# Low part of the next split weight tile given out ahead of the last step's evacuation

## The chip, the cores and the metric

The kernel runs on one core of one Trainium2 chip. The metric is the device time of one execution in microseconds (us), lower is better. Before the change it is 2506.51 us, the median of three runs (2506.17 to 2506.94).

## The reference

Two blocks over 256 tokens of width 2048, all in float32. Cut to what matters here:

```
# first block
proj   = rms_norm(x) @ w_in                       # 2048 -> 8192: q k v, h b c, z_conv z_attn
y_conv = rms_norm(b * conv3(c * h)) * silu(z_conv)
y_attn = rms_norm(attention(norm(q), norm(k), v)) * silu(z_attn)
x      = x + concat(y_conv, y_attn) @ w_out
# second block
proj   = rmsnorm(x) @ w_in_2                      # conv input, ssm input, two gates
conv   = silu(layernorm(conv31(glu))) @ conv_w_out_2
ssm    = (z @ w_val) * sigmoid(z @ w_gate),  z = gelu(scan of the grouped state space)
x      = x + (gate0 * conv + gate1 * ssm) @ w_out_2
h      = rmsnorm(x)
x      = x + peer(h)        # q = h @ w_q; top 16 of 128 x 128 keys; 16 experts' rows of u and v per head
out    = rmsnorm(x)
```

## The kernel before, in words

The 256 tokens stand on the free axis; the width is cut into rows of 128 partitions. The program goes through a list of 448 weight tiles of 128 x 2048 (1 MB each). The first 192 tiles are the projections; each of them is **split**. A raw tile comes by DMA on SP's queue into one of three buffers (RAW). ScalarE (ACT) copies it, rounded to fp32r, into one of three HI buffers: the high part (`w_hi`, L195). VectorE (DVE) subtracts that from the raw tile into one of two LO buffers: the low part (`w_lo`, L201). TensorE then multiplies high part by high input, high part by low input and low part by high input, which together give nearly the full float32 precision. The first two products stand in one matmul of 512 columns where the step is "wide" (L301, and L302 for the low part), or in three matmuls of 256 columns (L286 to L288, L277 to L279). The last 256 tiles (expert tables) are **whole**: their steps use the raw tile, without high or low part.

One tile is one step, given out by `step(mm, evac)` in one manually scheduled program, so each engine's queue has exactly the order in which the code gives the work out:

1. the pending evacuation of the step before, out of PSUM (`pend`);
2. `w_ahead(i)`: loads into free raw buffers, the low part of tile i+1 (with `LDL = 1`), the high part of tile i+2 (with `LDH = 2`);
3. the matmuls of step i;
4. a share of other work from generators (`weave`): attention, the state-space scan, the long convolution, square roots.

The load of tile i+4 goes out after the low part of tile i+1, whose raw buffer it takes. The low part of tile i+1 overwrites that of tile i-1, so it also waits for the matmuls of step i-1.

The evacuations differ by stage. In the wide steps `total` copies one half of the PSUM bank by ACT (L311) and adds the other half by DVE (L313):

- **query and key steps** (`ev_q`, `ev_k`; 16 of the first 24 tiles): L311, L313, then a square on ACT (L506, L521). For a key, later in the weave: square root on ACT (L530), reciprocal (L532) and scaling (L533) on DVE. Between them, `q_scale` (L562 on ACT, L564 and L565 on DVE).
- **value, h, c and b steps**: L311, L313, with nothing on ACT behind DVE for v and h; c multiplies (L627) and runs a three-tap convolution in the weave; b multiplies (L647) and squares on ACT (L649).
- **gated z steps** (`ev_z`, 16): L311, L313, scaling L668 beside silu on ACT (L666), product L670, then `split_to`: copy on ACT (L343), subtraction on DVE (L344).
- **residual steps** (`residual_step`, 16 in each block): L311, L313, addition L844, square on ACT (L850); in the second block also `split_x`: copy on ACT (L1147) and L1148 on DVE.
- **projections of the second block** (L1064 to L1078): ACT alone, or for glu ACT and then a product on DVE.
- **value-gate steps** (`ev_vg`): sigmoid on ACT (L1111), two products on DVE (L1112, L1113).
- **c-out steps** (`ev_co`, 8): twice product, addition (L1120, L1121) on DVE, copy on ACT (L343), subtraction on DVE (L344).
- **query projections of the last stage** (`ev_pq`): one product on DVE (L1166).

Of the kernel before, what the change touches and what calls it, by code (L numbers as in the profile page):

```python
# [123 lines left out]
def body(ctx, tc, xT, par, wst, kst, bblk, cblk, gfin, uexp, vexp, out):  # L124
# [28 lines left out]
    LDH, LDL = 2, 1  # L153
    WU = 192
    ws = {"n": 0, "dma": 0, "hi": 0, "lo": 0}
    order = []
# [8 lines left out]
    def raw_of(i):  # L165
        return RAW[i % 3] if i < WU else EARLY[i - WU] if i < WU + 3 else S[w_slot[i]]
# [11 lines left out]
    def w_release(i):  # L178

        k = w_slot.pop(i, None)  # L180
        if k is not None:
            w_free.append(k)
# [9 lines left out]
    def w_hi():  # L192
        i = ws["hi"]
        if i not in whole:
            nc.scalar.activation(hi_of(i), raw_of(i), AF.Copy)  # L195
        ws["hi"] += 1

    def w_lo():
        i = ws["lo"]
        if i not in whole:  # L200
            nc.vector.tensor_tensor(out=lo_of(i), in0=raw_of(i), in1=FV(hi_of(i)), op=ALU.subtract)  # L201
        ws["lo"] += 1

    def w_loads():
        while ws["dma"] < len(order) and raw_free(ws["dma"]):
            w_load()

    def w_ahead(i):

        last = len(order) - 1  # L210
        w_loads()
        while ws["lo"] <= min(i + LDL, last) and ws["dma"] > ws["lo"]:
            if ws["hi"] <= ws["lo"]:
                w_hi()
            w_lo()
            w_loads()
        while ws["hi"] <= min(i + LDH, last) and ws["dma"] > ws["hi"]:
            w_hi()

    plain = lambda raw: raw  # L220
    w_base = {"q": 32, "k": 40, "v": 48, "h": 0, "b": 8, "c": 16, "zc": 24, "za": 56}
# [29 lines left out]
    def step(mm, evac, budget=2600.0, fine=0.0):  # L251

        i = ws["n"]
        while pend:
            pend.pop(0)()
        w_ahead(i)
        parts = mm(raw_of(i)) if i in whole else mm(hi_of(i), lo_of(i))
        for _ in parts or ():
            weave.run_fine(fine)
        ws["n"] += 1  # L260
        if i in whole:
            w_release(i)
        pend.append(evac)
        weave.run(budget)
        weave.run_paced()
# [151 lines left out]
    def first_tiles(pss, xs, evs):  # L417

        i, n = ws["n"], len(pss)
        w_ahead(i)  # L420
        ws["n"] += n
        his, los = [[w[j % len(w)] for j in range(i, i + n)] for w in (HI, LO)]
        wk = lambda w, k: w[:, k * P:(k + 1) * P]
        late = list(range(1, KT, 2)) + list(range(0, KT, 2))
        jobs = [(his[t], t, k, 0) for k in range(KT) for t in range(2)]
        if n == 2:
            jobs = [j for k in range(KT) for j in ((his[0], 0, k, 0), (los[0], 0, k, 0), (his[1], 1, k, 0))]
            jobs += [(his[t], t, k, 1) for t in range(2) for k in late] + [(los[1], 1, k, 0) for k in range(KT)]
        else:
            jobs += [(his[t], t, k, 1) for k in late for t in range(2)]  # L430
            jobs += [(his[2], 2, k, p) for p in range(2) for k in range(KT)]
            jobs += [(los[t], t, k, 0) for t in range(3) for k in range(KT)]
        for q, (w, t, k, p) in enumerate(jobs):
            if ws["lo"] < i + n and t == 1 and w is los[1]:
                w_lo()
            rest = [u for _, u, _, _ in jobs[q + 1:]]
            nc.tensor.matmul(pss[t], wk(w, k), xs(k)[p], start=all(u != t for _, u, _, _ in jobs[:q]),  # L437
                             stop=t not in rest)
        if n == 3:
            w_hi()  # L440
            w_lo()
            w_loads()
        pend.extend(evs)
        weave.run(0)
# [375 lines left out]
    for kind, j in plan[3:]:  # L820
        ps = mmbank2(1)
        if kind == "k" and j == 0:
            weave.add(q_scale(), True)
        if kind == "h" and j == 0:
            for g in range(3):
                weave.add(attention(g), True)
        ev = {
            "q": lambda: ev_q(ps, j), "k": lambda: ev_k(ps, j), "v": lambda: ev_v(ps, j),
            "h": lambda: ev_copy(ps, sl(u_s, j)), "c": lambda: ev_c(ps, j), "b": lambda: ev_b(ps, j),
            "za": lambda: ev_z(ps, a_s, col["aog"], rbuf, j, 8 + j),  # L830
            "zc": lambda: ev_z(ps, u_s, col["cog"], rconv, j, j),
        }[kind]()
        if kind == "za" and j == 0:
            weave.drain()
            y_s = slots([18, 19, 20, 17], F32R)
            yv = hl_view(y_s)
        step(lambda wh, wl: mm_wide(ps, wh, wl, hl2(h_s), range(KT)), ev)
# [4 lines left out]
    def residual_step(ps, j, xsv, ysv, perm, then=lambda j: None, last=lambda f: f()):  # L842
        def ev():
            nc.vector.tensor_tensor(out=xsv(j), in0=total(ps), in1=xsv(j), op=ALU.add)  # L844
            if j == 0:
                nc.scalar.activation(sqsum, xsv(j), AF.Square)
                then(j)
                return
            sq = hold()
            nc.scalar.activation(sq, xsv(j), AF.Square)  # L850
            if j < KT - 1:
                nc.gpsimd.tensor_tensor(out=sqsum, in0=sqsum, in1=sq, op=ALU.add)  # L852
            then(j)
            if j == KT - 1:
                def f():
                    sum_tokens(sqsum, True, False)
                    sum_tokens(sq, False, True)
                    drop(sq)
                last(f)
            else:  # L860
                drop(sq)
        if j == KT - 1:
            need_sqrt()
        step(lambda wh, wl: mm_wide(ps, wh, wl, ysv, perm), ev)
# [221 lines left out]
    for j in range(2, 8):  # L1086
        ps = mmbank()
        step(proj(ps), ev_u(ps, j), mix())
# [635 lines left out]

    n0 = ws["n"]
    w_ahead(n0 + LAST - 1)
    ws["n"] += LAST
    zs = slots([9, 23])
# [113 lines left out]
```

## Time and profile before

| | |
|---|---|
| median of 3 runs | 2506.51 us |
| the profiled execution | 2509.01 us, of it the span from first to last instruction 2507.0 us |
| TensorE (PE) busy | 2405.0 us, 96% of the span |
| weight loads (PEld) busy | 2279.6 us |
| VectorE (DVE) busy | 1616.7 us |
| ScalarE (ACT) busy | 729.1 us |
| GpSimd (POOL) busy | 642.4 us |
| low part L201, 192 times | 453.3 us, 2362 ns each |
| high part L195, 192 times | 366.1 us, 1908 ns each |
| mean granted TensorE clock | 0.994 |

The split stages fill the first 1220 us or so; the rest are the steps with whole tiles. TensorE is busy nearly all the time, so what matters is what it waits for in the few per cent that are left, and whether VectorE and ScalarE have the next high and low parts ready when a step begins. In a timeline row the first number is the start in us, the second the duration; in brackets at its end is how long the engine sat idle before, and what ended that.

### The profile page before, as it was taken

To read this page: it belongs to the slowest core of one execution; us is meant where nothing else is said; L and a number is where in the kernel's file an instruction comes from. 1 tells how busy PE (TensorE), PEld (TensorE's weight loads), DVE (VectorE), ACT (ScalarE), POOL (GpSimd) and SP (SyncE) were. 2 spreads that over 40 slices of the span, in tenths; PEclk is the share of its full clock that TensorE was granted. 3 is DMA by queue.
4 is the path that set the end of the run, shared out by engine and by line. 5 is a ranking of instruction groups with operands and counts; after the bars stand their busy time and mean duration, and the time that the engine had idled before them with its cause. 6 is when DMAs were issued, how large, how long until landed. Compare 5 with 4: busy or idle time off the path is not lost.

```text
span 2507.0 us, 41129 instructions
## 1 busy us (share of the span) xinstructions
PE 2405.0 (96%) x17080; PEld 2279.6 (91%) x17080; DVE 1616.7 (64%) x2874; ACT 729.1 (29%) x1118; POOL 642.4 (26%) x845
## 2 busy tenths in 40 slices
PE   8999999999999999999999999999999899999987
PEld 7888878899999999989999899889988899998886
DVE  6857777589999987767897664453553431645542
ACT  5544454443235445453113940000000000000002
POOL 1788888410000000010131022212221320322110
PEclk9999999999999999999999999999999999999998
DMA  6455555565555545465799889999999999999993
GB/s 238 169 197 186 174 199 193 211 239 198 202 212 179 181 168 179 177 221 209 288 397 421 302 335 421 391 420 367 421 421 420 389 382 367 410 414 420 420 379 115
DMA packets 119323, 729.17 MB, mean 291 GB/s; under 512 B 13281, under 2 KB 25729, under 8 KB 35169
## 3 DMA queue, kind: packets, MB, share of 16 engines
q1 hardware_dynamic: 65760, 474.50, 49.9%
q0 software_dynamic: 34848, 231.85, 23.1%
q10 hardware_dynamic: 18528, 20.19, 2.5%
q8 instruction: 134, 2.20, 0.4%
q14 instruction: 53, 0.43, 0.0%
HBM read 703.33 MB, written 23.07 MB: 290 GB/s over the span
## 4 chain that ended last, share of the span: by engine, by line
PE 72%; DMA 18%; ACT 5%; DVE 4%; issue 1%; SPq 0%; ACTq 0%; DVEq 0%
PE b L1651 15%; DMA s<-in_vexp_dram 12%; PE b L1668 12%; PE b L301 11%; PE b L302 6%; PE b L286 6%; PE b L288 6%; PE b L287 6%; DMA s<-in_wst_dram 5%; DVE s L201 2%; PE b L279 2%; PE b L278 2%; PE b L277 2%; ACT s L1439 1%; PE b L437 1%; ACT s L1419 1%
## 5 line engine op out<-in xcount | busy, mean ns | idle before, releaser
L1668 PE MATMUL b<-s,s 128*128 128x160 f32 x4096 | 583.1, 301 | 32.2 <-DMA s<-in_vexp_dram 31.6
L1668 PEld LDWEIGHTS b<-s,s 128*128 128x128 f32 x4096 | 564.0, 191 | 46.8 <-issue 38.6
L1651 PE MATMUL b<-s,s 128*128 128x160 f32 x4096 | 580.5, 300 | 16.4 <-DMA s<-in_wst_dram 15.3
L1651 PEld LDWEIGHTS b<-s,s 128*128 128x128 f32 x4096 | 562.1, 190 | 30.0 <-issue 26.6
L301 PE MATMUL b<-s,s 128*128 128x512 f32 x1456 | 519.3, 400 | 0.0
L201 DVE TENSOR_TENSOR s<-s,s 128x2048 fp32r<-128x2048 f32 x192 | 453.3, 2362 | 24.4 <-issue 12.3
L302 PE MATMUL b<-s,s 128*128 128x256 f32 x1456 | 408.5, 281 | 9.6 <-DVE s L201 9.5
L195 ACT ACTIVATE s<-s 128x2048 fp32r<-128x2048 f32 x192 | 366.1, 1908 | 47.7 <-PE b L287 30.0
L1542 DVE SCALAR_TENSOR_TENSOR s<-s,sqsum,s 128x2048 f32<-128x2048 f32 x93 | 218.6, 2351 | 178.7 <-DMA s<-in_vexp_dram,rbuf 178.2
L301 PEld LDWEIGHTS b<-s,s 128*128 128x128 f32 x1456 | 273.4, 188 | 63.8
L286 PE MATMUL b<-s,s 128*128 128x256 f32 x1152 | 330.7, 287 | 0.0
L1527 DVE CUSTOM_DVE_ANT_0 s<-s,s 128x2048 f32<-128x2048 f32 x96 | 219.5, 2291 | 169.1 <-DMA s<-in_uexp_dram,rbuf 169.1
L288 PE MATMUL b<-s,s 128*128 128x256 f32 x1152 | 326.7, 284 | 0.0
L287 PE MATMUL b<-s,s 128*128 128x256 f32 x1152 | 326.6, 284 | 0.0
L302 PEld LDWEIGHTS b<-s,s 128*128 128x128 f32 x1456 | 274.7, 189 | 13.5 <-DVE s L201 12.8
L1654 ACT ACTIVATE s<-b 128x160 f32<-128x160 f32 x128 | 38.8, 303 | 774.7 <-PE b L1651 761.0
L1488 POOL DMA_INDIRECT s<-in_uexp_dram,rbuf x96 | 117.0, 1219 | 519.4 <-DVE s L1542 235.6
L286 PEld LDWEIGHTS b<-s,s 128*128 128x128 f32 x1152 | 221.6, 192 | 3.7 <-issue 2.9
L287 PEld LDWEIGHTS b<-s,s 128*128 128x128 f32 x1152 | 221.7, 192 | 0.3
L288 PEld LDWEIGHTS b<-s,s 128*128 128x128 f32 x1152 | 221.6, 192 | 0.0
L1488 POOL DMA_INDIRECT s<-in_vexp_dram,rbuf x96 | 116.6, 1215 | 343.4 <-DVE sqsum L1527 203.8
L852 POOL TENSOR_TENSOR sqsum<-sqsum,s 128x256 f32<-128x256 f32 x28 | 37.9, 1354 | 405.6 <-ACT s L850 405.5
(319 smaller groups left out, 2511.5 us busy)
## 6 DMA issues: line engine op xcount, KB each, us to landing
s<-in_wst_dram SPq DMA_DIRECT2D x320, 1024.0 KB
s<-in_vexp_dram SPq DMA_DIRECT2D x128, 1024.0 KB
tabd<-s POOLq DMA_DIRECT2D x32, 256.0 KB
s<-tabd ACTq DMA_DIRECT2D x32, 256.0 KB
gd<-s ACTq DMA_DIRECT2D x6, 1024.0 KB
s<-gd POOLq DMA_DIRECT2D x14, 384.0 KB
xd<-s POOLq DMA_DIRECT2D x4, 1024.0 KB
s<-in_bblk_dram ACTq DMA_DIRECT2D x8, 512.0 KB
```

Of the source, the lines that this page charges most:

```text
L195: nc.scalar.activation(hi_of(i), raw_of(i), AF.Copy)
L201: nc.vector.tensor_tensor(out=lo_of(i), in0=raw_of(i), in1=FV(hi_of(i)), op=ALU.subtract)
L286: nc.tensor.matmul(ps, a, xh, start=(j == 0), stop=False)
L287: nc.tensor.matmul(ps, a, xl, start=False, stop=False)
L288: nc.tensor.matmul(ps, b, xh, start=False, stop=(j == len(perm) - 1))
L301: nc.tensor.matmul(ps, a, x2, start=(j == 0), stop=False)
L302: nc.tensor.matmul(ps[:, :T], b, x2[:, :T], start=False, stop=(j == len(perm) - 1))
L1488: nc.gpsimd.indirect_dma_start(out=S[b][:], out_offset=None, in_=uexp if kind == "u" else vexp, in_offset=bass.IndirectOffsetOnAxis(ap=gad ...
L1527: V.tensor_tensor_reduce(out=buf, in0=buf, in1=x_rep, scale=1.0, scalar=0.0, op0=ALU.mult, op1=ALU.add, accum_out=dots_[:, k:k + 1])
L1542: V.scalar_tensor_tensor(out=acc_s, in0=buf, scalar=a, in1=acc_s, op0=ALU.mult, op1=ALU.add)
L1651: nc.tensor.matmul(ps, raw[:, k * P:(k + 1) * P], nv(k)[:, NS_:T], start=(k == 0), stop=(k == KT - 1))
L1668: nc.tensor.matmul(acc[d], raw[:, d * P:(d + 1) * P], act_at(i), start=False, stop=(i == P - 1 and (d % 3 == 2 or d == KT - 1)))
```

## The change

In `step` the low part is given out first, then the pending evacuation, then the rest of `w_ahead`, which is the high part. For that the loop over low parts gets a name of its own, `w_lows`; `w_ahead` calls it too and finds nothing left to do in it.

```diff
     def w_ahead(i):
 
+        w_lows(i)
+        last = len(order) - 1
+        while ws["hi"] <= min(i + LDH, last) and ws["dma"] > ws["hi"]:
+            w_hi()
+
+    def w_lows(i):
         last = len(order) - 1
         w_loads()
         while ws["lo"] <= min(i + LDL, last) and ws["dma"] > ws["lo"]:
@@
             w_lo()
             w_loads()
-        while ws["hi"] <= min(i + LDH, last) and ws["dma"] > ws["hi"]:
-            w_hi()
@@
     def step(mm, evac, budget=2600.0, fine=0.0):
 
         i = ws["n"]
+        w_lows(i)
         while pend:
             pend.pop(0)()
         w_ahead(i)
```

Lines behind `step` stand five lower in the changed kernel: L313 is L318 there, L1120 is L1125. L195 and L201 keep their numbers.

DVE's queue in the key steps, before (L201 is the low part, L313 the evacuation, L532 and L533 the reciprocal and scaling of an earlier key, L564 and L565 belong to the query scale):

```order
L564 RECIPROCAL small<-small 128x16
L565 TENSOR_SCALAR small<-small 128x16
L313 TENSOR_TENSOR s_117<-b_67,s_86 128x256
L201 TENSOR_TENSOR s_84<-s_78,s_81 128x2048
L532 RECIPROCAL s_86<-s_86 128x256
L533 SCALAR_TENSOR_TENSOR s_117<-s_117,small,s_86 128x256
L313 TENSOR_TENSOR s_117<-b_65,s_86 128x256
L201 TENSOR_TENSOR s_85<-s_79,s_82 128x2048
```

The same place in the changed kernel:

```order
L569 RECIPROCAL small<-small 128x16
L570 TENSOR_SCALAR small<-small 128x16
L201 TENSOR_TENSOR s_84<-s_78,s_81 128x2048
L318 TENSOR_TENSOR s_117<-b_67,s_86 128x256
L537 RECIPROCAL s_86<-s_86 128x256
L538 SCALAR_TENSOR_TENSOR s_117<-s_117,small,s_86 128x256
L201 TENSOR_TENSOR s_85<-s_79,s_82 128x2048
L318 TENSOR_TENSOR s_117<-b_65,s_86 128x256
```

The low part has moved ahead of the evacuation, behind the weave of the step before.

ACT's queue at that place in the changed kernel (L316 is the copy L311 of before, L526 the square L521, L195 the high part, L535 the square root L530):

```order
L316 ACTIVATE s_86<-b_67 128x256
L526 ACTIVATE s_87<-s_117 128x256
L195 ACTIVATE s_82<-s_79 128x2048
L535 ACTIVATE s_86<-b_68,small 128x256
L316 ACTIVATE s_86<-b_65 128x256
L526 ACTIVATE s_87<-s_117 128x256
```

Here nothing has moved: copy, square, high part, square root stand as they did.

DVE's queue in the c-out steps, before (L1120 product, L1121 addition, L344 subtraction behind ACT's copy L343):

```order
L201 TENSOR_TENSOR s_85<-s_78,s_81 128x2048
L1120 TENSOR_TENSOR s_4303<-b_66,s_4303 128x256
L1121 TENSOR_TENSOR s_4303<-s_4303,s_4305 128x256
L344 TENSOR_TENSOR s_108<-s_4303,s_108 128x256
L1120 TENSOR_TENSOR s_4303<-b_67,s_4303 128x256
L1121 TENSOR_TENSOR s_4303<-s_4303,s_4305 128x256
L344 TENSOR_TENSOR s_108<-s_4303,s_108 128x256
L201 TENSOR_TENSOR s_84<-s_79,s_82 128x2048
```

and in the changed kernel:

```order
L201 TENSOR_TENSOR s_84<-s_79,s_82 128x2048
L1125 TENSOR_TENSOR s_4303<-b_66,s_4303 128x256
L1126 TENSOR_TENSOR s_4303<-s_4303,s_4305 128x256
L349 TENSOR_TENSOR s_108<-s_4303,s_108 128x256
L1125 TENSOR_TENSOR s_4303<-b_67,s_4303 128x256
L1126 TENSOR_TENSOR s_4303<-s_4303,s_4305 128x256
L349 TENSOR_TENSOR s_108<-s_4303,s_108 128x256
L201 TENSOR_TENSOR s_85<-s_80,s_83 128x2048
```

The low part that stood behind all six operations of an evacuation (`s_84<-s_79,s_82`) stands ahead of them.

## Rows read from the trace of the kernel before

**Rows 1.** List of waits: engine, line, released by; us in total, times, longest.

```profile
PE b L302 <- DVE s L201: 9.5, 9, 2.1
PEld b L302 <- DVE s L201: 12.8, 10, 2.4
```

**Rows 2.** Busy time by stage: length, PE, PEld, DVE, ACT, POOL, clock, DMA share, GB/s.

```profile
220.00:281.00 61.00, 58.28 (x335) 50.60 (x333) 53.60 (x79) 29.57 (x55) 52.99 (x71) 1.00 0.49 173
325.00:424.00 99.00, 92.84 (x519) 79.19 (x518) 76.07 (x87) 52.98 (x69) 85.60 (x143) 1.00 0.56 192
985.00:1120.00 135.00, 135.00 (x901) 123.78 (x900) 96.11 (x118) 69.20 (x87) 10.88 (x15) 1.00 0.51 185
```

**Rows 3.** Timeline of DVE in one c-out step.

```profile
991.56 2.29 DVE L201 TENSOR_TENSOR s<-s,s 128x2048 fp32r<-128x2048 f32 x1
993.76 0.42 DVE L1120 TENSOR_TENSOR s<-b,s 128x256 f32<-128x256 f32 x1
994.21 0.42 DVE L1121 TENSOR_TENSOR s<-s,s 128x256 f32<-128x256 f32 x1
...
996.06 0.43 DVE L1121 TENSOR_TENSOR s<-s,s 128x256 f32<-128x256 f32 x1
...
997.32 2.29 DVE L201 TENSOR_TENSOR s<-s,s 128x2048 fp32r<-128x2048 f32 x1
```

**Rows 4.** Timeline of ACT in one key step.

```profile
104.83 1.91 ACT L195 ACTIVATE s<-s 128x2048 fp32r<-128x2048 f32 x1
106.64 0.45 ACT L530 ACTIVATE s<-b,small 128x256 f32<-128x256 f32 x1
```

**Rows 5.** Timeline of DVE in the same key step.

```profile
104.04 0.42 DVE L313 TENSOR_TENSOR s<-b,s 128x256 f32<-128x256 f32 x1 [0.63 <-ACT s L311]
104.39 2.28 DVE L201 TENSOR_TENSOR s<-s,s 128x2048 fp32r<-128x2048 f32 x1
107.12 1.75 DVE L532 RECIPROCAL s<-s 128x256 f32<-128x256 f32 x1 [0.46 <-ACT s L530]
108.91 0.48 DVE L533 SCALAR_TENSOR_TENSOR s<-s,small,s 128x256 f32<-128x256 f32 x1
110.02 0.42 DVE L313 TENSOR_TENSOR s<-b,s 128x256 f32<-128x256 f32 x1 [0.63 <-ACT s L311]
```

**Rows 6.** Timeline of DVE in the key step with the query scale.

```profile
80.43 2.83 DVE L201 TENSOR_TENSOR s<-s,s 128x2048 fp32r<-128x2048 f32 x1
84.55 0.25 DVE L564 RECIPROCAL small<-small 128x16 f32<-128x16 f32 x1 [1.29 <-ACT small L562]
```

**Rows 7.** Timeline of DVE in one gated z step.

```profile
372.23 0.42 DVE L313 TENSOR_TENSOR s<-b,s 128x256 f32<-128x256 f32 x1 [1.12 <-ACT s L311]
...
373.15 0.43 DVE L670 TENSOR_TENSOR s<-s,s 128x256 f32<-128x256 f32 x1
...
377.89 0.42 DVE L313 TENSOR_TENSOR s<-b,s 128x256 f32<-128x256 f32 x1 [0.93 <-ACT s L311]
```

**Rows 8.** Timeline of ACT in the c-out step of rows 3.

```profile
996.52 0.42 ACT L343 ACTIVATE s<-s 128x256 fp32r<-128x256 f32 x1 [1.44 <-DVE s L1121]
996.85 1.90 ACT L195 ACTIVATE s<-s 128x2048 fp32r<-128x2048 f32 x1
```

**Rows 9.** Groups of DVE instructions in 325 to 424 us: busy, mean ns, idle before.

```profile
L201 DVE TENSOR_TENSOR s<-s,s 128x2048 fp32r<-128x2048 f32 x17 | 43.1, 2537 | 0.0
L670 DVE TENSOR_TENSOR s<-s,s 128x256 f32<-128x256 f32 x16 | 9.9, 617 | 3.0 <-ACT s L666 1.6
...
L355 DVE RECIPROCAL rconv<-rconv 128x256 f32<-128x256 f32 x1 | 1.7, 1740 | 0.0
```

**Rows 10.** Timeline of ACT in one residual step of the second block.

```profile
1099.40 0.42 ACT L850 ACTIVATE s<-s 128x256 f32<-128x256 f32 x1 [1.01 <-DVE s L844]
1099.73 0.49 ACT L1147 ACTIVATE s<-s,prm 128x256 fp32r<-128x256 f32 x1
1100.13 1.90 ACT L195 ACTIVATE s<-s 128x2048 fp32r<-128x2048 f32 x1
```

## The prediction

> **What bounds the kernel now.** I read the list of waits first, then the busy time by stage, then the timelines of VectorE (DVE) and ScalarE (ACT) in the stages of the split weights. The low part of a weight tile (L201) keeps TensorE waiting for 9.5 us at its products (L302), and the weight-load row of the same product shows 12.8 us [rows 1]. That is all this change can win. By stage nearly all of it lies in two places: 2.7 us of TensorE idle in 220 to 281 us and 6.2 us in 325 to 424 us, while in 985 to 1120 us TensorE has no idle time, 135.00 of 135 us [rows 2]. The granted clock is 1.00 in all these stretches, the 2.4 GHz level, so waits of this size did not cost clock.
>
> So where the low part is late today, there is a gain; elsewhere the question is whether the new order makes something late that is not.
>
> **What the change does to the queues.** Before, a step's queues read, on DVE: evacuation of the step before, low part of the next tile; on ACT: evacuation, high part of the tile after next. Both parts hung on the evacuation side by side. Now DVE reads: low part, evacuation; ACT is unchanged. Where the evacuation has an ACT operation that needs a DVE result, this closes a **loop**: low part, DVE part of the evacuation, ACT part, high part behind it in ACT's queue, and the next step's low part needs that high part. If one turn of the loop is longer than a step's products, every further step runs at the loop's length, once the slack is used. The slack is a step less one low part: the low part may start that late and still be done when the next step begins.
>
> Each turn below is added up from start-to-start distances. A low part holds DVE for 2.20 us (991.56 to 993.76) [rows 3]; a high part takes 1.91 us [rows 4], and the next low part starts at its end.
>
> **Part by part.**
>
> Query and key steps. A query evacuation turns in 2.20, then L313 to L195 0.79 (the square of the new row stands between them), then 1.91: 4.9 us against a step of 5.98 (L313 at 104.04 to L313 at 110.02) [rows 4, 5]. No loss. In six key steps DVE has the reciprocal of an earlier key between evacuation and next low part, and that waits for a square root (L530) which stands behind the high part on ACT. The turn: 2.20 + 0.79 + 1.81 (L195 to L530) + 0.48 (L530 to L532) + 1.79 (L532 to L533) + about 0.4 to the next = 7.47 us, so 1.49 us over the step, six times 8.9 us. Slack: 5.98 - 2.28 = 3.7. The chain may come in late already. In the step before, L564 waits for ACT and starts 4.12 us behind the low part, which is 3.68 behind the high part (that starts 0.44 behind the low part) [rows 4 to 6]. In the new order it would start 2.20 + 0.79 + 3.68 = 6.7 behind the low part, the next low part half a microsecond later, 1.2 us late, and 1.8 if that low part is stretched to 2.83 as in its row [rows 6]. I take 2: 2 + 8.9 - 3.7 = **7.2 us lost**, ends 5.2 (no lateness) and 8.2 (3 us).
>
> Value, h and c steps. The evacuation's first ACT copy needs only TensorE and the high part follows it at once: no loop. In 220 to 281 us the low part no longer stands behind a copy on ACT and one or two DVE operations. I take the whole idle time as won, **-2.7**, ends 0 and -3.5 (the wait counted by the weight-load row, a third more).
>
> Gated z steps (16, in 325 to 424 us). Turn: 2.20, L313 to L670 0.92, L670 to its ACT copy 0.46 and copy to L195 0.33 (as from L1121 to the same copy L343 in the c-out steps), 1.91: 5.82 us, against a step of 5.66 (372.23 to 377.89) [rows 7, 8]. But DVE is stretched here: mean low part 2.54 instead of 2.28, mean L670 0.62 instead of 0.43 [rows 7, 9]. So a turn is 6.27, and 16 turns are 100.3; a reciprocal of 1.74 [rows 9] stands once between an evacuation and the next low part, mostly beside the high part, and I put 1.2 on the stage for it and for what belongs to it, an estimate. The unstalled products are 92.8 (the busy time) [rows 2]. With half a microsecond of slack left on entering, as the square root of the attention norm stands ahead of the low part there, the stall is 101.5 - 92.8 - 0.5 = 8.2, in place of today's 6.2: **+2**, ends -3 (full slack and half the stretch) and +10 (the stretch grows).
>
> The Trainium skill, GPSIMD Engine Reference, section Key points, says that GpSimd shares its SBUF interfaces with VectorE and contends with DVE instructions that have two SBUF inputs, which the low part is. The stretched rows agree, where POOL is busy for 85.6 of 99 us [rows 2]. Without the stretch the stage would stand at 16 x 5.82 + 1.2 - 92.8 - 0.5 = 1 us of stall, and the sum 7 us lower.
>
> First residual steps. Turn without stretch 2.20 + 0.46 + 0.46 + 0.33 + 1.91 = 5.4, under the step. The first three are still stretched and enter with no slack: 3 x (5.4 + 0.5 - 5.65) and some more: **+1**, ends 0 and 3.
>
> Second block. Its projections evacuate by ACT alone, or by ACT first and DVE behind, so no loop and no DVE operation that the low part overtakes: 0. The same for the value-gate steps.
>
> c-out steps (8 evacuations). The turn is 2.20, L1120 to L1121 0.45, first L1121 to the second 1.85 (a copy on ACT and the subtraction behind it stand between), 0.46 to ACT's copy L343, 0.33 to L195, 1.91: 7.20 us against 5.76 (991.56 to 997.32) [rows 3, 8]. Over by 1.44, eight times 11.5, slack 3.5: **+8.0**, ends 6 and 9. Today TensorE waits for nothing here.
>
> Second residual steps. Turn: 2.20 + 0.46 + 0.46 + 0.33 (L850 to L1147) + 0.40 (L1147 to L195) + 1.91 = 5.76 [rows 10], over by 0.1, and the slack is gone when they begin: 15 times, 1.5, with the turn that joins both stages **+2**, ends 0 and 4.
>
> The rest. Query projections of the last stage have DVE alone in the evacuation: 0. In the 256 steps with whole tiles there is neither part; the loads stand on SP in the same order as before: 0. SP's and POOL's orders do not change; a weight load goes out when its low part is done, so it moves with it, by up to 3.7 us, into queues that are half used (share 0.49 to 0.56) [rows 2], and its high part is two steps away. Twice, behind the hand-ordered first tiles, a high part now precedes the evacuations on ACT: 0, ends 0 and 1.9.
>
> **Sum:** 7.2 - 2.7 + 2 + 1 + 8.0 + 2 = 17.5, say +18 us on the profiled execution, which took 2509.0 (span 2507.0): 2527. The median of the runs shown is 2506.5, 2.5 lower, so **2524.5 us**. The later half is not a place where this comes back: its first loads of whole tiles and its gathers hang on the end of the split stages.
>
> **The rivals.**
>
> *The waits go and no loop closes* (faster). High parts are given out two tiles ahead; if DVE reaches the low part early enough in each turn, that lead is never used up. Then the price is rows 1 alone: 2506.5 - 9.5 = 2497, down to 2494. It decides at a turn equal to the step: the z turn without stretch is only 0.16 over, the residual 0.1. Against it: key and c-out are 1.4 to 1.5 over, and ACT's order keeps the high part behind the evacuation. Chance 0.08.
>
> *The z stage wins after all.* Its stall vanishes to a third because the operations that were stretched meet POOL at another time: -4 there, the first residual steps 0, the second ones 0.5: 7.2 - 2.7 - 4 + 8 + 0.5 = 9, so 2515. For it: the bare z turn. Chance 0.2.
>
> *More stretch.* POOL's work stays where it is in time, and the low part now starts with the step; it could meet that work in more steps of the first block. If all six key turns and all 16 z turns paid the 0.55 us of the low part at 80.43 [rows 6] in place of the means: 3.3 and 16 x 0.3 = 4.8, with both residual stages at their upper ends 4 more: +12, so 2536. Against it: in the key steps the row at 104.39 has 2.28 [rows 5]. This is where the rule of the Trainium skill cited above would take the time if it held in every step. Chance 0.12.
>
> *It cancels* (within 0.2%): loops as said in c-out, but key steps enter early and both gains are at their ends: 5.2 - 3.5 - 3 + 6 = 4.7, so 2511. Chance 0.05.
>
> **How the numbers follow.** The forecast (2518 to 2532) has the rest, 0.55. A measurement of this kernel can tell about 0.2%, 5 us. The range, 2510 to 2537, holds the forecast, the z rival, most of the contention and half of the cancelling; it leaves out the faster one and the tails. Faster 0.08, same 0.05, slower 0.87, all from these cases.
>
> **What would show it.** Right: TensorE's waits for L201 grow from 9.5 to about 28 us; in the key steps from the fourth on, and in the c-out steps from the third or fourth, the step is 7.2 to 7.5 us long and DVE idles before L201 waiting for ACT's high part, a wait that hardly exists today. The idle in 220 to 281 us is gone. Wrong: c-out steps still at 5.76 us (then the high part is not held back, and the first rival holds), or a second block between 530 and 890 us whose length changes (then I missed an evacuation there).

## The result, and the profile after

| | before | changed |
|---|---|---|
| median | 2506.73 us (2506.17 to 2511.53, 4 runs) | **2539.8 us** (2537.09 to 2545.35, 4 runs) |
| ratio, 95% interval | | 1.0129 [1.0114, 1.0144] |
| the profiled execution, its span | 2509.01, 2507.0 us | 2545.35, 2541.7 us |

Slower, as forecast, but by 33 us where 18 were forecast: 2.8 us beyond the upper end of the range. The profiled execution of the changed kernel is its longest run; a second profile of it (below) has a span of 2533.7. Differences of a few us between single executions are therefore told as such. The change was measured once more in a later batch (e6): 2536.59 us, 0.4 below the upper end of the range and 27 above the kernel before beside it. So the forecast loss of 18 us was too small in both batches, while the range was just missed in one and just met in the other. Two single executions far beyond all others, 4030.78 us in e3 and 6216.8 us of the kernel before, stand in no median of this text.

The page of the changed kernel, the span and the lines of TensorE (PE) and of the low part:

```profile
span 2541.7 us, 41273 instructions
...
PE 2418.1 (95%) x17080; PEld 2288.0 (90%) x17080; DVE 1610.7 (63%) x2874; ACT 723.5 (28%) x1118; POOL 609.6 (24%) x845
...
L201 DVE TENSOR_TENSOR s<-s,s 128x2048 fp32r<-128x2048 f32 x192 | 448.7, 2338 | 212.9 <-issue 67.8
```

The work is the same (17080 matmuls, 192 low parts), and the low part is even a little shorter: 448.7 us against 453.3. What is new is that DVE idles 212.9 us in front of it; before it was 24.4. By itself that says nothing, since DVE is not the bound. The list of waits of PE up to 1300 us says what of it reaches the end:

```profile
PE b L307 <- DVE s L201: 16.8, 15, 2.2
...
PE b L306 <- DVE s L349: 7.0, 3, 3.2
...
PE b L282 <- DVE s L1125: 3.3, 3, 1.2
...
PE b L306 <- DVE s L1125: 1.1, 1, 1.1
```

The first row answers to [rows 1], 9.5 us before. It grew to 16.8, not to 28; but two names stand beside it that the list of before does not have: L349, the subtraction with which an evacuation ends, and L1125, the DVE operation that frees a PSUM bank. All four rows together are 28.2 us (26.2 in the second profile). The same list for DVE, with the wait that the forecast was about:

```profile
DVE s L201 <- ACT s L195: 51.4, 40, 2.8
DVE s L537 <- ACT s L535: 15.9, 6, 2.6
```

Forty low parts now wait for their own high part, the edge with which the loop closes. The stages of [rows 2] in the changed kernel:

```profile
220.00:281.00 61.00, 61.00 (x356) 53.71 (x355) 50.49 (x82) 32.35 (x62) 45.59 (x72) 1.00 0.57 205
325.00:424.00 99.00, 90.68 (x493) 76.41 (x492) 73.26 (x82) 46.15 (x62) 86.52 (x131) 0.98 0.49 173
985.00:1120.00 135.00, 126.34 (x854) 116.24 (x853) 86.68 (x113) 63.37 (x87) 6.65 (x9) 0.97 0.47 168
```

The idle time of 220 to 281 is gone. In the last row PE has 8.66 us without work where it had none, and the clock is 0.97, where it was 1.00 (the same times, but by then the changed kernel is 14 to 27 us behind in its work).

**The loss, stage by stage.** All 187 step beginnings of the split stages can be matched between two traces by the first product of each step. How this is read, at both ends of the second block (before, then changed):

```profile
528.75 0.28 PE L286 MATMUL b<-s,s 128*128 128x256 f32 x1
...
886.45 0.28 PE L277 MATMUL b<-s,s 128*128 128x256 f32 x1
```

```profile
544.08 0.28 PE L291 MATMUL b<-s,s 128*128 128x256 f32 x1
...
901.73 0.28 PE L282 MATMUL b<-s,s 128*128 128x256 f32 x1
```

The changed kernel is 15.33 us behind at the first pair and 15.28 at the second, so 357.7 us of second block cost nothing. Below is what each stage adds to the lag, by such pairs (in brackets the time in the trace of before). "Again" is the second profile of the changed kernel.

| stage | forecast | changed | again |
|---|---|---|---|
| up to the middle of the query and key steps (to 97.7) | 0 | +0.8 | +0.4 |
| key steps (to 139.3) | +7.2 | +8.9 | +9.1 |
| value, h, c, b (to 326.2) | -2.7 | -4.0 | -4.0 |
| gated z (to 413.4) | +2 | +3.2 | +0.8 |
| last z evacuation and first residual (to 504.3) | +1 | +5.4 | +5.1 |
| norm and first tiles of the second block (to 536.1) | 0 | +0.9 | +0.6 |
| second block and value gate (to 977.1) | 0 | 0.0 | 0.0 |
| c-out (to 1030.0) | +8.0 | +4.3 | +4.3 |
| second residual (to 1114.8) | +2 | +7.3 | +5.4 |
| norm, query projections (to 1221.4) | 0 | +1.2 | +2.4 |
| steps with whole tiles | 0 | +6.7 | +2.8 |
| sum | +17.5 | +34.7 | +26.7 |

### The profile page after: what moved, and what is told of

It reads as the page before. It is cut to its first block, busy times and chain, and to the rows that moved or that the text cites. A ratio compares the mean times of both kernels' runs of the same rounds, so it can differ in the third digit from the quotient of the medians.

```text
span 2541.7 us, 41273 instructions
## 1 busy us (share of the span) xinstructions
PE 2418.1 (95%) x17080; PEld 2288.0 (90%) x17080; DVE 1610.7 (63%) x2874; ACT 723.5 (28%) x1118; POOL 609.6 (24%) x845
## 4 chain that ended last, share of the span: by engine, by line
PE 62%; DMA 20%; DVE 8%; ACT 8%; issue 2%; ACTq 0%; SPq 0%; DVEq 0%
PE b L1656 15%; DMA s<-in_vexp_dram 12%; PE b L1673 12%; PE b L306 8%; DMA s<-in_wst_dram 7%; PE b L291 5%; PE b L292 5%; PE b L293 5%; DVE s L201 4%; PE b L307 4%; ACT s L195 3%; ACT s L1444 1%; PE b L284 1%; PE b L283 1%; PE b L282 1%
## 5 line engine op out<-in xcount | busy, mean ns | idle before, releaser
L1656 PE MATMUL b<-s,s 128*128 128x160 f32 x4096 | 582.6, 301 | 18.3 <-DMA s<-in_wst_dram 17.9
L201 DVE TENSOR_TENSOR s<-s,s 128x2048 fp32r<-128x2048 f32 x192 | 448.7, 2338 | 212.9 <-issue 67.8
L307 PE MATMUL b<-s,s 128*128 128x256 f32 x1456 | 411.5, 283 | 16.8 <-DVE s L201 16.8
L195 ACT ACTIVATE s<-s 128x2048 fp32r<-128x2048 f32 x192 | 365.7, 1905 | 52.5 <-PE b L292 30.0
L857 POOL TENSOR_TENSOR sqsum<-sqsum,s 128x256 f32<-128x256 f32 x28 | 20.7, 740 | 464.8 <-ACT s L855 464.8
```

The source lines that it names most:

```text
L307: nc.tensor.matmul(ps[:, :T], b, x2[:, :T], start=False, stop=(j == len(perm) - 1))
L1656: nc.tensor.matmul(ps, raw[:, k * P:(k + 1) * P], nv(k)[:, NS_:T], start=(k == 0), stop=(k == KT - 1))
```

## The experiments

The theory is that of the prediction: low part, DVE part of the evacuation, ACT part, high part and the next low part form a loop, and where its turn is longer than a step the steps run at the turn's length. The rivals that came up are named where they are tried. Numbers in the text are medians; lags come from the profiled execution, matched as above. The kernel before ran beside each batch: 2507.35 (e1 to e4), 2509.16 (e5 to e8), 2508.05 (e9 to e11) and 2508.46 us (e12).

**e1, the loop opened.** Low and high part both stand ahead of the evacuation, in every step, so the high part no longer waits for it.

```diff
         i = ws["n"]
-        w_lows(i)
+        w_ahead(i)
         while pend:
             pend.pop(0)()
-        w_ahead(i)
```

> Low part and high part both ahead of the pending evacuation, in every split step. Theory (the loss comes from a loop: the high part stands on ACT behind an evacuation that now waits for the low part on DVE): the loop is open, so the key steps are 5.98 us and the c-out steps 5.76 us again, no wait of TensorE for the low part in the z steps, and the time falls to 2497 to 2501 us, faster than before the change by the waits of rows 1. Rival (it is the evacuation itself that is late, by the 2.2 us of the low part, and TensorE waits for its PSUM bank or its results): the loss stays, 2530 us or more, and the evacuations on ACT are later still by the 1.9 us of a high part.

Measured: 2514.09, ratio 1.003 [1.002, 1.004]. The lag at the last split step is 4.7 us instead of 24 to 28. Waits of PE:

```profile
PE b L305 <- ACT s L322: 4.9, 1, 4.9
PE b L290 <- ACT s L1068: 4.1, 1, 4.1
PE b L306 <- DVE s L201: 3.0, 1, 3.0
```

The many waits for L201 and those for the PSUM bank are gone, and of those for the subtraction 0.6 us are left (line numbers in this kernel are one smaller). The loop is open, but the time is above the 2497 to 2501 of the theory. What is left are three single waits: one for a low part in the z steps, and two directly behind the hand-written first tiles of each block, where a high part now stands ahead of the evacuation on ACT, and the step behind waits for that evacuation. So the low part's own place is not what costs; it is the high part behind the evacuation.

**e2, the low part ahead for value, h and c alone**, where no loop was forecast. A flag, set behind each step of the first block by its kind, guards the early low part:

```diff
-        w_lows(i)
+        if lead[0]:
+            w_lows(i)
...
+        lead[0] = kind in ("v", "h", "c")
```

> Low part ahead only of the evacuations of value, h and c steps, where the high part does not hang on DVE; all other steps as before the change. Theory: the 4.6 us that these stages win in the changed kernel's trace stay, and nothing is lost: about 2502 us. Rival (a part of the loss comes with any move of the split stages, as the later half, bound by DMA, took 5 to 7 us more): 2506 to 2509 us.

Measured: 2506.48, 0.9997 [0.9987, 1.0006]; the lag is -2.7 behind the b steps and -4.9 at the end of the split stages. The gain is there in the trace of the split stages. In the median only 0.9 us of it are seen, which is within the noise and what the rival expected; in the profile the part with whole tiles is 1.8 us longer, and where the rest went is not shown.

**e3, e4, e5: the old order back in one group of steps**, the rest as in the change. The same flag: in e3 `kind not in ("q", "k")`; in e4 set to false behind the first c-out step and left so, in the second residual stage too; in e5 `kind not in ("za", "zc")`, true again in the residual steps.

> The change, without the query and key steps, which are as before. Theory: the loop of the key steps costs 9.1 us in the changed kernel's trace, and these come back: 2530.7 us against 2539.8. Rival (the delay is eaten by slack later or is part of what the later half adds): 2537 us or more.

> The change up to the first c-out step; c-out steps, second residual steps and query projections as before. Theory: 13.6 us come back, of them 8 from the c-out loop, 4 from the turn into the residual steps (there the products wait for the last c-out evacuation) and 2 from the residual loop: 2526 us. Rival (the prediction's term of 10 us): 2530 us.

> The change, without the steps that evacuate a gated z tile, which are as before. Theory (the loop of the z stage costs much more than the prediction's 3 us with the residual steps behind it: between the low parts at its ends the trace of the changed kernel has 8.6 us more): 8 to 9 us come back, 2530 to 2532. Rival (the term was right, and the extra time of that stage is lateness that the residual steps give back anyway): 3 us, 2536 to 2537.

Measured: 2528.21 (1.0088 [1.0073, 1.0104]), 2523.54 (1.0066 [1.0051, 1.0080]) and 2532.89 (1.0098 [1.0081, 1.0116]). By lag: in e3 the key steps add 0.1 us instead of 8.9. In e4 everything from the second c-out step to the last split step adds -0.1 us, where the change adds 12.9 to 13.7: half the loss of the split stages arises in c-out and the steps behind it. In e5 z and first residual steps still add 3.6 us (5.7 to 9.3), against 5.9 to 8.6. That is the weakest of the three, and the theory's 8 to 9 us did not come back: beside the change in the same batch (2536.59) it is 3.7 us, near the rival's 3. Turning the order back in the middle puts one low part behind an evacuation when it is late already, and PE waits 4.4 us for it.

**e6, the change once more**, for the spread of single profiles (the column "again" above).

> The changed kernel itself, once more. In its first trace the part behind the last low part took 1296.9 us, against 1290.0 before and 1290.2 to 1291.8 in four variants that start that part up to 19 us later. Theory (that part is not lengthened by the change, its time varies from run to run): the part takes 1290 to 1293 us and the median is 2535 to 2538. Rival (a delay of 28 us does lengthen it, for the order in which its loads meet the gathers): again 1295 us or more, and 2540.

Measured: 2536.59 (2535.12 to 2545.8), 1.0123 [1.0102, 1.0144]. The part behind the last low part takes 1293.0 us, at the upper end of what the theory said.

**e7 and e8, a version that beats both.** e7 is e1 but for the steps directly behind the first tiles, which keep the old order. e8 gives the low part alone ahead for v, h and c, low and high part for z, and leaves the rest as it was:

```diff
+        if lead[0] == "low":
+            w_lows(i)
+        elif lead[0] == "both":
+            w_ahead(i)
+        lead[0] = ""
...
+        lead[0] = {"v": "low", "h": "low", "c": "low", "za": "both", "zc": "both"}.get(kind, "")
```

> Both parts ahead of the evacuation, but not in the two steps directly behind the hand-ordered first tiles, where the trace of the variant with both parts ahead shows TensorE waiting 4.9 and 4.1 us for an evacuation on ACT that stands behind a high part. Theory: these 9 us come back, 2505 us, with the loop open in all stages. Rival (the rest of that variant's loss is the high part ahead of every evacuation on ACT): 2510 us or more.

> By stage: low part ahead behind value, h and c tiles, both parts ahead behind gated z tiles, all else as before the change. Theory: 4.9 us from the first (as the trace of that variant shows), 3 to 5 more from the z stage, where the variant with both parts ahead has one wait of 3.0 us left of 6.2: 2498 to 2500 us. Rival (the z stage is bound by VectorE itself, whatever the order): 2503 us.

Measured: e7 2500.35 (2498.38 to 2507.66), 0.9967 [0.9953, 0.9981]; e8 2501.76 (2495.06 to 2507.36), 0.9971 [0.9957, 0.9985]. Lags at the last split step: -5.7 and -6.8. In e8 the low part is waited for like this:

```profile
PE b L312 <- DVE s L201: 3.7, 2, 3.4
```

Of the 9.5 us that stood to be won [rows 1] 5.8 are won, once the high part does not stand in the loop.

**e9, the PSUM banks.** In the change PE waits 4.4 us for L1125, which frees a bank; a rival for the c-out loss is that the four banks run out. Eight banks from the c-out steps on:

```diff
+        banks[:] = [0, 1, 2, 3, 4, 5, 6, 7]
```

> The change, with eight PSUM banks in turn instead of four in the c-out steps and the second residual steps. In the changed kernel TensorE waits four times about 1.1 us for the product that empties a PSUM bank (L1125) and then 4.2 us for the last subtraction of the stage (L349). Theory (the loop sets when the last evacuation is done, and the first residual step needs its result; the bank waits only take some of that time earlier): the four bank waits go, the wait for L349 grows to about 8 us, and the time stays within 2 us of the changed kernel. Rival (the banks are a cost of their own): 4 us come back.

Measured: 2538.91, 1.0114 [1.0099, 1.0130]. Waits of PE, with those for L1125 gone:

```profile
PE b L307 <- DVE s L201: 14.4, 17, 1.6
PE b L306 <- DVE s L349: 8.8, 3, 4.1
...
PE b L284 <- DVE s L201: 2.6, 3, 1.1
```

The c-out steps lose 1.9 us less, and the first two residual steps behind them 1.8 to 2.3 more (9.1 against 7.3 and 6.7). The wait for L349 behind c-out is 4.70 us, against 4.25 in the change, and not the 8 that the theory expected: the low part (L284 in the rows above) now takes most of the bank waits' place. The banks are not the cause; they are one of the names under which the loop's lateness shows.

**e10, a pure delay.** The kernel before with 112 products of 512 columns added in the second residual stage, their result unused: does the part with whole tiles get longer merely because it starts later?

```diff
+        if j == 2:
+            for n in range(112):
+                nc.tensor.matmul(B[7], h_s[n % 4][:, 0:P], h_s[n % 4][:, 512:1024], start=True, stop=True)
```

> The kernel before, with 112 more matmuls of 512 columns behind the third residual step of the second block, into an unused PSUM bank: some 24 to 26 us during which TensorE does nothing for the output, and no order changed. Theory (the part behind the last low part does not depend on when it starts): that part takes 1290 to 1292 us and the kernel loses just the delay. Rival (a delay of this size lengthens it): 1293 us or more.

Measured: 2533.62, 1.0104 [1.0087, 1.0121]; the lag behind it is 24.1 us, and the steps with whole tiles add 0.5 more in its profile. A delay goes through to the end, nothing is won back and little added.

**e11, the kernel before in the same batch**, one execution.

> The kernel before itself, for a second profile. Theory: the last low part starts at 1217 us to within 1 us, the waits for L201 are the same ten or so, and the part behind it takes 1288 to 1292 us. Rival (stages vary by several us from run to run, as the two profiles of the changed kernel differ by 4 us at the last low part): 2 us or more off.

Measured: 2508.22, span 2506.2. At the last split step it stands at -0.2 us against the first profile of it, and the part behind is 0.6 shorter.

**e12, the order undone at two steps only**: in the first step of each residual stage the evacuation goes ahead of the low part again.

```diff
+        lead[0] = j > 0
         step(lambda wh, wl: mm_wide(ps, wh, wl, ysv, perm), ev)
+        lead[0] = True
```

> The order of the changed kernel everywhere, except in the first step of each residual stage, where the last evacuation (of the last gated z step, of the last c-out step) goes ahead of the low part again. Theory A, the evacuation has a deadline of its own, which the prediction left out: the products of that step need its result, and the low part ahead of it delays it by 2.2 us. Then the 8.1 us that TensorE waits for the subtraction behind the copy (L349) fall to under 4, the lag at the last low part falls from 23.7 to 16 to 20 us, and the time to about 2530. Theory B, the lateness of the loop is a fixed sum and only shows under another name there: the wait moves to the low part of the next step (6 us or more for L201 on top of 13.7), the lag stays at 23 to 24 and the time at 2535 to 2539.

Measured: 2534.22 (2532.26 to 2536.49), 1.0102 [1.0085, 1.0119], between the two expectations, as is the lag at the last split step, 22.7 us. Waits of PE:

```profile
PE b L310 <- DVE s L201: 18.4, 18, 1.5
...
PE b L309 <- DVE s L352: 3.3, 2, 2.2
```

(L352 is the subtraction L349 of the change.) Behind c-out the first two residual steps add 3.2 us instead of 6.7 to 7.3. TensorE's wait there falls from 4.25 us for the subtraction to 1.16 for it and 1.35 for the next low part: the evacuation does have a deadline of its own, but nearly half of what that gives back goes to the other name. Behind the z steps the four steps from 413.4 on add 7.2 instead of 6.4 to 6.7: there nothing is won, the wait is 2.18 us for the subtraction and 1.34 for the low part, where the two profiles of the change have 2.75 and 4.11 for the subtraction alone. A second thing differs. The clock behind the c-out steps, in the change and then in e12:

```profile
1056.00:1060.00 4.00, 1.14 (x3) 0.67 (x4) 2.48 (x7) 1.78 (x3) 0.00 (x0) 0.77 0.65 233
1060.00:1064.00 4.00, 4.00 (x13) 3.38 (x13) 3.05 (x3) 1.12 (x2) 0.00 (x0) 0.50 0.07 29
```

```profile
1056.00:1060.00 4.00, 2.65 (x16) 2.35 (x16) 3.97 (x4) 0.64 (x2) 0.00 (x0) 1.00 0.34 98
1060.00:1064.00 4.00, 4.00 (x25) 3.55 (x24) 1.74 (x3) 3.01 (x4) 0.00 (x0) 1.00 1.02 383
```

In the change the granted clock falls to 0.50, the 1.2 GHz level, behind waits of 3.25 and 1.00 us, and its mean from 1056 to 1066 us is 0.66; in e12, where no wait there is over 1.4 us, it stays at 1.00. So of the 3.5 to 4.1 us won there about 3.4 (10 us less 34%, an estimate) are clock, and the wait alone is worth less than 2.

## Why the prediction was wrong in size

In short: the waits grew by about what was forecast, and the step that failed is "waits of this size did not cost clock", by which the sum has no term for the clock. Behind the places where the loop's lateness comes due the clock fell, and up to the last split step the products themselves took 8.9 us longer (6.1 in the second profile). By stage two more terms were mis-sized, and their errors partly cancel.

**Right: the loop, its turns, and where there is none.** The key steps of the changed kernel, on DVE:

```profile
80.53 3.23 DVE L201 TENSOR_TENSOR s<-s,s 128x2048 fp32r<-128x2048 f32 x1 [2.83 <-ACT s L195]
83.69 0.41 DVE L318 TENSOR_TENSOR s<-b,s 128x256 f32<-128x256 f32 x1
88.13 0.26 DVE L569 RECIPROCAL small<-small 128x16 f32<-128x16 f32 x1 [4.03 <-ACT small L567]
88.42 1.51 DVE L570 TENSOR_SCALAR small<-small 128x16 f32<-128x16 f32 x1
89.84 2.28 DVE L201 TENSOR_TENSOR s<-s,s 128x2048 fp32r<-128x2048 f32 x1
92.05 0.41 DVE L318 TENSOR_TENSOR s<-b,s 128x256 f32<-128x256 f32 x1
95.10 1.75 DVE L537 RECIPROCAL s<-s 128x256 f32<-128x256 f32 x1 [2.65 <-ACT s L535]
96.89 0.48 DVE L538 SCALAR_TENSOR_TENSOR s<-s,small,s 128x256 f32<-128x256 f32 x1
97.29 2.30 DVE L201 TENSOR_TENSOR s<-s,s 128x2048 fp32r<-128x2048 f32 x1
...
104.76 2.34 DVE L201 TENSOR_TENSOR s<-s,s 128x2048 fp32r<-128x2048 f32 x1
```

From low part to low part 7.45 and 7.47 us; 7.47 was forecast. A c-out turn:

```profile
1039.66 2.29 DVE L201 TENSOR_TENSOR s<-s,s 128x2048 fp32r<-128x2048 f32 x1 [1.31 <-ACT s L195]
1041.87 0.42 DVE L1125 TENSOR_TENSOR s<-b,s 128x256 f32<-128x256 f32 x1
...
1046.74 2.29 DVE L201 TENSOR_TENSOR s<-s,s 128x2048 fp32r<-128x2048 f32 x1 [1.31 <-ACT s L195]
```

7.08 us, 7.20 forecast; DVE stands idle 1.31 us for the high part. The z turn without stretch is 5.84 (from 428.59 to 434.43), 5.82 forecast. The second block adds 0.0, the idle time of 220 to 281 is gone, and the first rival (no loop) fell with e1, where the loop's opening takes away 20 us.

**Too small: how late the key chain comes in.** The mis-sized term is "I take 2". From the low part at 80.53 to the next at 89.84 are 9.31 us, 3.3 over a step of 5.98. The 3.68 from high part to reciprocal was right (84.45 to 88.13). But the low part took 3.23, not 2.83, and L570, a 128x16 operation of 0.23 us in the trace of before, took 1.51. By the prediction's own formula 3.3 + 8.9 - 3.7 = 8.5; measured 8.9 to 9.1. The gain in value, h, c and b was also larger, -4.0, beyond its end of -3.5.

**Wrong: the end of the loop.** By stage the largest miss in the split steps is the term "second residual ... with the turn that joins both stages +2", and the same joint in "first residual +1". The prediction counted one deadline only, that of the low part, and took the lateness in c-out as eight turns less the slack. The c-out steps themselves lost less than that: the first four lose nothing, the later ones 1.2 to 1.4 each, 5.2 together (4.3 in the table, which takes in a gain of 1.0 in the step ahead of them). But the loop also makes the evacuation late, and the first residual step needs its result. PE in that step:

```profile
1057.86 0.55 PE L306 MATMUL b<-s,s 128*128 128x512 f32 x1 [3.25 <-DVE s L349]
1058.21 0.42 PE L307 MATMUL b<-s,s 128*128 128x256 f32 x1
1059.63 0.79 PE L306 MATMUL b<-s,s 128*128 128x512 f32 x1 [1.00 <-DVE s L349]
1060.22 0.41 PE L307 MATMUL b<-s,s 128*128 128x256 f32 x1
1060.43 0.63 PE L306 MATMUL b<-s,s 128*128 128x512 f32 x1
...
1061.07 0.63 PE L306 MATMUL b<-s,s 128*128 128x512 f32 x1
```

Lateness that the slack had hidden through the c-out steps came due at once: 4.25 us of waiting. Behind it a pair of products starts every 0.64 us (1060.43 to 1061.07), where e12 has 0.35 there (1057.58 to 1057.93). c-out and second residual together: 11.6 and 9.7 us by the table, against 10 forecast; the sum of the two terms was nearly right, by errors that cancel, and about 3.4 us of what was measured are clock. In e4 both vanish together, and in e9 and e12 one part of the lateness moves to another name. Behind the z steps the same joint was put at +1 and cost 5.1 to 5.4, and 7.2 over four steps when the order was undone there. TensorE waits there for the same subtraction, 2.75 us at 438.95 (4.11 in the second profile), but that the evacuation's place behind the low part is the cause is not shown: e12 speaks against it. Stretched operations stand there (L675 takes 1.34 us at 424.97, 0.42 at 431.72), and the clock is 0.79 from 436 to 444 in the change and in e12, 1.00 before.

**Left out: the clock, and the norm.** The prediction said that waits of this size did not cost clock, and put it at nothing. PE's busy time up to the last split step and behind it, the same products in both kernels, before and then in the change:

```profile
0.00:1221.38 1221.38, 1193.83 (x8445) 1107.02 (x8445) 957.64 (x1392) 559.08 (x703) 376.74 (x595) 1.00 0.56 198
1221.38:2507.00 1285.62, 1211.19 (x8639) 1172.62 (x8637) 659.05 (x1483) 169.99 (x415) 265.68 (x250) 0.99 0.95 379
```

```profile
0.00:1249.42 1249.42, 1202.74 (x8445) 1111.74 (x8445) 951.59 (x1392) 553.96 (x703) 345.21 (x595) 0.99 0.54 194
1249.42:2541.70 1292.28, 1215.40 (x8639) 1176.25 (x8637) 659.11 (x1483) 169.54 (x415) 264.36 (x250) 0.99 0.94 377
```

Of the 28.0 us of lag 19.1 are time without a product (46.7 less 27.6), where the sum has 17.5; the other 8.9 are products that take longer. In the second profile it is 17.9 and 6.1. The granted clock stands at 0.50 for 23.9 us of this part in the change (20.5 in the second profile) and for 6.8 before (10.2 in e11). At half the clock about half of such time is lost (pairs every 0.64 us instead of 0.35), so 8.5 and 6.8 us more than in the first profile of before are an estimate of what it took. Two of these places stand in both profiles of the change and in neither of the kernel before: behind the z steps (0.79 from 436 to 444) and behind c-out (0.66 from 1056 to 1066 in the first), together about 5 us. The 0.98 in 325 to 424 is not one of them: the second profile of the change has 1.00 there, while e11, which is the kernel before, falls to 0.88 from 346 to 360, behind a wait of 2.42 us for a low part. So the prediction's sentence did not hold in every execution of the kernel before either. The norm and query projections behind the second residual add 1.2 to 2.4 us instead of 0.

**In part open: the steps with whole tiles.** They were put at 0. In the four profiles with the low part alone ahead in all stages (changed, again, e9, e12) they are 6.7, 2.8, 5.4 and 4.8 us longer than in the first profile of before; in e7, where nothing is late, also 4.4; in the other eight -0.6 to 1.8. The delay by itself does not do it (e10, 0.5). By the rows above the 6.7 are 2.5 us more without a product and 4.2 of longer products; the time at 0.50 is 4.4 us longer there, so about 2.2 of it are clock. In e12 TensorE idles 0.7 us more in this part and by the same estimate the clock costs 4.8 more, in e7 0.8 and 3.9. But in e2 and e8 the clock costs over 3 us more too, with parts that are only 1.8 and 0.1 us longer. Why the clock falls there more often, and whether the change causes it, was not found.

**The rivals and the range.** Cancelling, and the z stage that wins after all, fell with the table. "More stretch" came nearest in time (2536), but not by its mechanism. It priced every key turn with a stretched low part; the low parts from 89.84 on take 2.28 to 2.34 us, with POOL at work beside them. Of the key steps only the one at 80.53 paid.

From profile to profile the miss is 17.2 us (34.7 less 17.5). By the table it is: key +1.7, value to b -1.3, z +1.2, the two residual stages +4.4 and +5.3, c-out -3.7, the two norms +0.9 and +1.2, the start +0.8, the whole tiles +6.7. The range had to hold the joints, the clock behind them and the last of these, and it held none. That the sum of the waits came out near 17.5 is in part luck: the z joint was 4 us too small, and c-out with the residual steps behind it 2 too large.

## What to carry to other kernels

When work is moved ahead in an in-order queue, draw the cycle that goes through both queues and back, and compare its turn with the step; where it closes and the helper and its predecessor are on different engines, move both ahead or neither, as e7 did, and e8 in the z steps; where it does not close (v, h and c in e8), the one alone can go ahead. Lateness that slack hides is not gone: look for the first consumer behind the stage that needs the loop's other result, since there it all comes due, and where it does, the clock can fall: price that too. Waits under new names (a bank, a subtraction) may be the same lateness; to tell, remove one and see whether another grows by as much.

## What was not expected of the hardware

The contention of DVE and POOL does not look like a slower rate for both; one of them waits until the other is done. L570, an operation of 128x16, took 1.51 us in one profile of the change and 1.52 in the other, and its counterpart before 0.23, as DVE's timeline of the kernel before has it:

```profile
84.83 0.23 DVE L565 TENSOR_SCALAR small<-small 128x16 f32<-128x16 f32 x1
```

POOL's timeline in the changed kernel; its first row ends at 89.90, and L570 beside it at 89.93:

```profile
87.49 2.41 POOL L777 TENSOR_TENSOR s<-s,s 128x1024 f32<-128x1024 f32 x1
...
97.53 2.17 POOL L797 TENSOR_TENSOR s<-s 128x32 f32<-128x32 f32 x1
99.66 0.25 POOL L798 TENSOR_TENSOR s<-s 128x32 f32<-128x32 f32 x1
...
421.40 3.18 POOL L816 TENSOR_TENSOR s<-s,s 128x512 f32<-128x512 f32 x1
```

The other way round, L797 of POOL has 128x32 elements, like L798 with 0.25 us, and takes 2.17 while the low part of 97.29 runs, to within 0.1 us of its end at 99.59. L816 takes 3.18 us beside the low part of 421.39 (2.29 us), and the one of the same shape ahead of it 1.22. The low part of 80.53 fits as well: POOL's L774 (79.22 to 81.61) was under way when it started, and it took 3.23 us, 0.95 more than the 2.28 of the one at 89.84. So a low part that comes first stays at 2.3 us beside a busy POOL in these rows. The Trainium skill (Trainium Architecture — The Big Picture, section What this means for kernel authors) calls the port pair that DVE and GpSimd share an exclusive lock, not a bandwidth split; these rows agree, though no run here tried it by itself. By these rows a stretch should be priced by which operation starts first and how much of it is left, not by a mean.

The second is the clock. Waits of about 1 us, one in each of four steps running (the last three of c-out and the first residual), left it at 1.00, and the 3.25 and 1.00 us behind each other took it to 0.50. A single wait can be enough: in the changed kernel 2.20 us for a low part at 347.20 were followed by 0.50 from 349 to 351 us, while 2.08 us at 353.30 left it at 1.00 in the first profile of the kernel before.
